# 112 of the 256 pairs are searched, and the gates' reads from DRAM begin four steps later with five steps up to their use

## The chip, the cores and the metric

One NeuronCore of a Trainium2 chip runs one program. The metric is the device time of one execution in microseconds (us). The engines are named as in the profile: PE multiplies matrices, DVE works on vectors, ACT applies functions and copies, POOL issues gathers and some copies, SP issues DMAs, each in the order of its own instructions. They meet at semaphores.

## The reference, cut to what matters

Two transformer blocks on 256 tokens of width 2048. The change lies in the last part of the second block, a product-key expert layer: for each token and each of 8 heads, two lists of 128 scores are cut to the 16 best each, the sums of all 16 x 16 pairs are formed, the 16 best sums are kept, and their softmax weighs 16 of 16384 experts.

```python
sub = jnp.einsum("bshpk,hpnk->bshpn", q, peer_keys).astype(jnp.float32)
s, i = lax.top_k(sub, PEER_TOPK)
cand = (s[..., 0, :, None] + s[..., 1, None, :]).reshape(B, S, PEER_HEADS, PEER_TOPK * PEER_TOPK)
cidx = (i[..., 0, :, None] * N_KEYS + i[..., 1, None, :]).reshape(B, S, PEER_HEADS, PEER_TOPK * PEER_TOPK)
top_s, pos = lax.top_k(cand, PEER_TOPK)
idx = jnp.take_along_axis(cidx, pos, axis=-1)
gate = jax.nn.softmax(top_s, axis=-1).astype(h.dtype)
...
u = jnp.take(peer_u, i_blk, axis=0)
a = jax.nn.gelu(jnp.einsum("td,thkd->thk", x_blk, u)) * g_blk
v = jnp.take(peer_v, i_blk, axis=0)
return jnp.einsum("thk,thkd->td", a, v)
```

Both lists come out of `top_k` in falling order. Pair (a, c), counted from 0, is beaten by every pair with both places no worse, so it can be among the best 16 only where (a+1)(c+1) is at most 16.

## The kernel before, in words

All weights pass through one pipeline. A weight tile `raw` of 1 MB is loaded by SP (L208); ACT rounds half of it to `whi` (L130), DVE forms the rest `wlo = raw - whi` (L131), and PE multiplies with both (L263). Such a half is a piece: in the passes below a piece is 10 matmuls of 512 columns. There are three `raw` tiles and four pairs of `whi` and `wlo`, and a piece is prepared three pieces ahead of its matmuls (`LOOK = 3`).

The dense part of the expert layer multiplies with all experts. A group is 8 pieces (512 experts), a pass U(e) is 4 groups, and its output goes through GELU into a ring (`turn`, L1624 to L1627). After U(0) to U(3) passes V(0), U(4), V(1), ... follow. The gate of every expert multiplies the ring before its V pass. Half of the tokens' second tile goes another way, by gathered rows (`sparse`, L1576 to L1598).

Side work is written as Python generators. After each piece `tick` lets every running generator go `rate` steps on; a step ends at a `yield`. So the order of all instructions is fixed when the program is built, in pieces, and does not depend on time. These matter here:

- `lists_gen` (rate 1) finds the 16 best of each list, with `top16` (L1474 to L1478): five DVE instructions, each over the whole list.
- `top_gen` (rate 1.3) forms the sums (L1513), searches them head by head with `top16`, and finds the two places of each winner by comparing with 0 to 15, multiplying and summing (L1531, L1534, L1536), once for each of two halves of the tokens.
- `g_gen` (rate 0.8) turns the winners into a gate for every expert and writes them to DRAM, `scratch`, in 24 blocks through ACT (L1678) and POOL (L1679).
- `r_gen(e)` reads the gates of V pass e back in three parts of 512 KB (L1687, issued by SP) into one tile `t`, and multiplies the ring with each (L1692, DVE). Reads and multiplies alternate; the next `r_gen` begins when the one before has ended.
- `sparse` begins at the same tick as the first `r_gen`. Its L1576 makes an operand that SP copies between partitions (L1577); then it gathers rows (POOL, L1581) and reduces them (DVE, L1596).

Of the kernel before, what the change touches and what calls it, by code (L numbers as in the profile page):

```python
# [8 lines left out]
H16 = mybir.dt.float16  # L9
# [3 lines left out]
OP = mybir.AluOpType  # L13
# [44 lines left out]
class Builder:  # L58
# [21 lines left out]
    def H(self, i, key, dt=FT):  # L80

        s, n = (i // 2, 4096) if i >= 8 else (10 + i, 2048)
        if self.halves.get(s, (None,))[0] != key:
            self.halves[s] = key, self.pool.tile([128, n], dt, name=f"s{s}_{key}", tag=f"s{s}")
        o = 2048 * (i % 2) if i >= 8 else 0
        return self.halves[s][1][:, o:o + 2048]
# [850 lines left out]
def phase3(b, C, W, gs, X, ident, transposes, residual, norm_of, stat2, act_pair, lhs_of, res_need, bcast, jits,  # L937
# [6 lines left out]
    V, A, G, PE = nc.vector, nc.scalar, nc.gpsimd, nc.tensor  # L944
# [493 lines left out]
    def post_pq(n):  # L1438
        def f(p):
            if n == 0:  # L1440
                for h in range(2):
                    gs["res3", h].drain()
                norm_of(r3, ss3)
                nc.gpsimd.dma_start(H(16, "k")[:, :], d["keysT"])
                for r, lo in ((rd, 0), (rsp, 64)):
                    for o in (0, 64):
                        nc.gpsimd.dma_start(r[o:o + 64, :], r3[lo:lo + 64, 1:2])
                nc.gpsimd.dma_start(fold, d["fold"])
            for h in range(2):
                A.activation(Qp(n, h), b.ps[p.banks[h][0]][:, :], AF.Copy, scale=r3[:, h:h + 1])  # L1450
            gs["key", n] = b.start(key_gen(n))
            gs["lists", n] = b.start(lists_gen(n))
            if n == 2:
                gs["fuse"] = b.start(fuse())
            if n == 3:
                gs["top"] = b.start(top_gen(), 1.3)
        return f
# [7 lines left out]
    iota = C("iota")  # L1465

    def sarr16():

        t = H(7, "g")[:, 1024:2048].bitcast(H16)
        return (t[:, 0:256], t[:, 256:512], t[:, 512:1024].rearrange("p (q t) -> p q t", q=2),  # L1470
                t[:, 1024:1280].rearrange("p (n t) -> p n t", t=2))

    def top16(vals, idx, src, tmp):
        V.max(vals[:, 0:8], src)  # L1474
        V.max_index(idx[:, 0:8], vals[:, 0:8], src)
        V.match_replace(tmp, vals[:, 0:8], src, -3.0e38)
        V.max(vals[:, 8:16], tmp)
        V.max_index(idx[:, 8:16], vals[:, 8:16], tmp)  # L1478

    def found():  # L1480

        t = H(12, "top")
        return t[:, 0:512], t[:, 512:1024].bitcast(U32), t[:, 1024:1536], [t[:, 1536 + i * 256:1792 + i * 256] for i in range(2)]
# [11 lines left out]
    def top_gen():  # L1495
        V16, I16, If, rep = found()
        while not gs["lists", 3].done:
            yield
        V.tensor_copy(If, I16)
        yield  # L1500
        t8 = H(8, "sub")
        T16 = t8[:, 0:128]
        Pi, Pa, Pb = (t8[:, k * 128:k * 128 + 128].bitcast(U32) for k in (1, 2, 3))
        Fa, Fb, E = t8[:, 512:640], t8[:, 640:768], t8[:, 768:1152]
        sm = t8[:, 1152:1160]
        cand, eq = H(16, "k")[:, :], H(17, "k")[:, :]
        i1, i2, g12, it2 = sarr16()
        V.tensor_copy(it2, iota[:, :, None].to_broadcast([128, 128, 2]))
        for h in range(2):
            v4 = V16[:, h * 256:h * 256 + 256].rearrange("p (m q k) -> p m q k", m=8, q=2)  # L1510
            f4 = If[:, h * 256:h * 256 + 256].rearrange("p (m q k) -> p m q k", m=8, q=2)
            for m in (0, 4):
                V.tensor_tensor(cand[:, m * 256:m * 256 + 1024].rearrange("p (m a c) -> p m a c", m=4, a=16),  # L1513
                                v4[:, m:m + 4, 0, :, None].to_broadcast([128, 4, 16, 16]),
                                v4[:, m:m + 4, 1, None, :].to_broadcast([128, 4, 16, 16]), op=OP.add)
                yield
            for m in range(8):
                top16(T16[:, m * 16:m * 16 + 16], Pi[:, m * 16:m * 16 + 16], cand[:, m * 256:m * 256 + 256],
                      rep[m % 2])
                yield  # L1520
            V.tensor_scalar(Pa, Pi, 4, None, op0=OP.logical_shift_right)
            V.tensor_scalar(Pb, Pi, 15, None, op0=OP.bitwise_and)
            V.tensor_copy(Fa, Pa)
            V.tensor_copy(Fb, Pb)
            yield
            for q, F in enumerate((Fa, Fb)):
                for m in (0, 4):
                    e1 = eq[:, m * 256:m * 256 + 1024]
                    e3 = e1.rearrange("p (s a) -> p s a", a=16)
                    e4 = e1.rearrange("p (m s a) -> p m s a", m=4, s=16)  # L1530
                    V.tensor_tensor(e3, F[:, m * 16:m * 16 + 64, None].to_broadcast([128, 64, 16]),  # L1531
                                    iota[:, None, 0:16].to_broadcast([128, 64, 16]), op=OP.is_equal)
                    yield
                    V.tensor_tensor(e4, e4, f4[:, m:m + 4, q, None, :].to_broadcast([128, 4, 16, 16]), op=OP.mult)  # L1534
                    yield
                    V.tensor_reduce(E[:, q * 128 + m * 16:q * 128 + m * 16 + 64], e3, axis=AX.X, op=OP.add)  # L1536
                    yield
            g = E[:, 256:384].rearrange("p (m s) -> p m s", m=8)
            t3 = T16.rearrange("p (m s) -> p m s", m=8)
            V.tensor_tensor(g, t3, t3[:, :, 0:1].to_broadcast([128, 8, 16]), op=OP.subtract)  # L1540
            A.activation(g, g, AF.Exp)
            V.tensor_reduce(sm, g, axis=AX.X, op=OP.add)
            V.reciprocal(sm, sm)
            V.tensor_tensor(g, g, sm[:, :, None].to_broadcast([128, 8, 16]), op=OP.mult)
            if h:
                t = t8[:, 1160:1288].bitcast(I32)
                V.scalar_tensor_tensor(t, E[:, 0:128], 128.0, E[:, 128:256], op0=OP.mult, op1=OP.add)
                V.tensor_copy(which[64:128], t[64:128, 0:64])
                V.tensor_copy(share[64:128], E[64:128, 256:320])
                nc.gpsimd.dma_start(which[0:64], t[64:128, 64:128])  # L1550
                nc.gpsimd.dma_start(share[0:64], E[64:128, 320:384])
            for _ in range(4):
                yield
            p = b.bank()
            for k in range(3):
                PE.transpose(p[:, k * 128:k * 128 + 128], E[:, k * 128:k * 128 + 128], ident)
            s = slice(h * 128, h * 128 + 128)
            V.tensor_copy(i1[:, s], p[:, 0:128])
            V.tensor_copy(i2[:, s], p[:, 128:256])
            V.tensor_scalar(g12[:, 0, s], p[:, 256:384], GSCALE, None, op0=OP.mult)  # L1560
            V.scalar_tensor_tensor(g12[:, 1, s], p[:, 256:384], GSCALE, g12[:, 0, s], op0=OP.mult, op1=OP.subtract)
            yield
        gs["G"] = b.start(g_gen(), GATE_RATE)
# [42 lines left out]
    def ring(e, h):  # L1606

        j = e % 4
        return v3(H(14 + j // 2, "rc")[:, j % 2 * 1024:j % 2 * 1024 + 1024] if h else H(10 + j, "ra")[:, :], 16)
# [20 lines left out]
    def post_U(n):  # L1630

        def f(p):
            if n and ("s", n - 1) in gs:
                gs["s", n - 1].drain()
            for h in range(2):
                A.activation(GT(h), b.ps[p.banks[h][0]][:, :], AF.Copy, scale=rd if h else r3[:, 0:1])
            gs["s", n] = b.start(turn(n))
            if n % 4 == 3:
                gs["R", n // 4] = b.start(r_gen(n // 4))
        return f  # L1640
# [41 lines left out]
    def r_gen(e):  # L1682
        while not (gs["s", 4 * e + 3].done and "G" in gs and gs["G"].done and (e == 0 or gs["R", e - 1].done)):
            yield
        t = H(7, "g")[:, 1024:2048]
        for j in range(3):
            nc.sync.dma_start(t.rearrange("p (k m) -> p k m", k=8),  # L1687
                              b.scratch[8 * j:8 * j + 8, :, 128 * e:128 * e + 128].rearrange("k p m -> p k m"))
            for _ in range(5 if e else 3):
                yield  # L1690
            R = ring(e, j // 2)[:, :, j % 2 * 64:j % 2 * 64 + 64].rearrange("p n (k t) -> p k n t", k=8)
            V.tensor_tensor(R, R, t.rearrange("p (k n t) -> p k n t", k=8, n=16), op=OP.mult)  # L1692
            yield
# [217 lines left out]
```

## Time and profile before

| what | us |
|---|---|
| median of 3 runs | 3228.13 |
| lowest and highest | 3226.35, 3237.43 |
| profiled execution, its own time | 3225.99 |
| its span, first to last instruction | 3224.2 |
| PE busy in it | 3142.5 |
| DVE busy in it | 2249.8 |
| ACT busy in it | 1674.1 |

Busy times are sums over the whole span, and the stages have different limits. The passes U(0) to U(3) lie at about 1895 to 2280 us, the search by `top_gen` at about 1930 to 2050, `g_gen` at about 2050 to 2165, and the reads of the gates from 2171 on.

### The profile page before, as it was taken

Reading aid. Unit: us, or ns where it says so; the run is one execution under the profiler, and the core shown is the slowest. Engines: PE = TensorE matmul, PEld = TensorE weight load, DVE = VectorE, ACT = ScalarE, POOL = GpSimd, SP = SyncE. Lnnn points to the kernel's source line nnn. Section 1 sums busy time; section 2 is a strip of 40 time slices with the busy share of each in tenths; the row PEclk is TensorE's granted clock in tenths of the full one; section 3 lists DMA queues with packets and bytes.
Section 4 is the critical chain, followed back from the end, with each engine's and each line's share of the span. In section 5 each row is a group of like instructions: output and inputs, shape, how many; then the busy total and the mean of one; then the engine's idle time right before and its main releaser. Section 6 shows DMA issues by size and latency. Waiting matters only on the chain.

```text
span 3224.2 us, 37826 instructions
## 1 busy us (share of the span) xinstructions
PE 3142.5 (97%) x14264; PEld 2464.3 (76%) x14264; DVE 2249.8 (70%) x2963; ACT 1674.1 (52%) x2374; POOL 375.7 (12%) x252
## 2 busy tenths in 40 slices
PE   8799999999999999999999998998999999999998
PEld 6677778888888888877787886776777777777776
DVE  6986554444555555654455589987989899999975
ACT  5356454444454455455544554684445554555554
POOL 1011110000000010000000200012121232422300
PEclk9899999999999999999999999999999999999999
DMA  6444455455555546444355554689999999999964
GB/s 230 159 173 169 170 186 183 180 183 183 186 192 184 191 153 220 183 150 151 136 189 180 189 178 170 235 281 347 389 377 383 390 371 398 374 402 368 365 222 163
DMA packets 135239, 768.52 MB, mean 238 GB/s; under 512 B 13008, under 2 KB 38016, under 8 KB 47568
## 3 DMA queue, kind: packets, MB, share of 16 engines
q1 hardware_dynamic: 110000, 604.81, 51.7%
q0 software_dynamic: 24768, 160.25, 12.6%
q8 instruction: 111, 1.82, 0.2%
q10 hardware_dynamic: 288, 1.05, 0.1%
q14 instruction: 72, 0.59, 0.0%
HBM read 750.82 MB, written 14.68 MB: 237 GB/s over the span
## 4 chain that ended last, share of the span: by engine, by line
PE 83%; DVE 9%; DMA 4%; issue 2%; ACT 2%; POOL 0%; SPq 0%; POOLq 0%; ACTq 0%; DVEq 0%
PE ps L263 77%; DVE wlo L131 3%; DVE s_conv L511 1%; DMA raw<-in_peer_u 1%; DMA s_g<-scratch 1%; PE ps L476 1%; ACT whi L130 1%; DMA raw<-in_peer_v 1%; PE ps L1251 1%; PE ps L1624 0%; DMA raw<-in_w_in 0%; PE ps L1250 0%; DVE s_gb L1596 0%; DVE s_x L717 0%; PE ps L1676 0%
## 5 line engine op out<-in xcount | busy, mean ns | idle before, releaser
L131 DVE TENSOR_TENSOR wlo<-raw,whi 128x1024 fp32r<-128x1024 f32 (+2 forms) x1101 | 1330.9, 1217 | 792.5 <-ACT whi L130 787.1
L130 ACT ACTIVATE whi<-raw 128x1024 fp32r<-128x1024 f32 (+2 forms) x1113 | 1164.8, 1051 | 1035.5 <-PE ps L263 729.9
L263 PE MATMUL ps<-whi,s_x 128*128 128x512 f32 (+2 forms) x2816 | 903.2, 396 | 10.7 <-ACT whi L130 6.3
L263 PEld LDWEIGHTS ps<-whi,s_x 128*128 128x128 f32 x2816 | 529.4, 189 | 136.7 <-issue 8.2
L263 PE MATMUL ps<-whi,s_h 128*128 128x512 f32 x1760 | 608.4, 402 | 0.0
L263 PE MATMUL ps<-wlo,s_x 128*128 128x512 f32 (+2 forms) x1408 | 551.8, 392 | 16.8 <-DVE wlo L131 16.8
L263 PE MATMUL ps<-whi,s_vj 128*128 128x512 f32 x1536 | 530.6, 400 | 3.5 <-DVE s_vj L131 2.3
L263 PE MATMUL ps<-wlo,s_h 128*128 128x512 f32 (+1 forms) x1136 | 453.8, 400 | 20.2 <-DVE wlo L131 19.9
L263 PEld LDWEIGHTS ps<-whi,s_h 128*128 128x128 f32 x1760 | 333.8, 190 | 100.1 <-issue 0.8
L263 PE MATMUL ps<-wlo,s_vj 128*128 128x512 f32 (+1 forms) x1024 | 403.9, 394 | 0.2 <-DVE wlo L131 0.2
L263 PEld LDWEIGHTS ps<-whi,s_vj 128*128 128x128 f32 x1536 | 289.3, 189 | 104.8 <-DVE s_vj L131 4.4
L263 PEld LDWEIGHTS ps<-wlo,s_x 128*128 128x128 f32 x1408 | 266.0, 189 | 75.0 <-DVE wlo L131 18.5
L263 PE MATMUL ps<-whi,s_fj 128*128 128x512 f32 x1024 | 322.0, 395 | 0.0
L263 PEld LDWEIGHTS ps<-wlo,s_h 128*128 128x128 f32 (+1 forms) x1136 | 187.4, 165 | 75.0 <-DVE wlo L131 28.2
L263 PEld LDWEIGHTS ps<-whi,s_fj 128*128 128x128 f32 x1024 | 192.2, 188 | 47.4
L263 PE MATMUL ps<-wlo,s_fj 128*128 128x512 f32 x512 | 202.4, 395 | 0.0
L263 PEld LDWEIGHTS ps<-wlo,s_vj 128*128 128x128 f32 (+1 forms) x1024 | 165.1, 161 | 45.8 <-DVE wlo L131 1.3
L1581 POOL DMA_INDIRECT s_k<-in_v_rows,vec x43 | 112.4, 2613 | 208.4 <-DVE s_sp L1598 190.3
L131 POOL TENSOR_TENSOR s_head<-raw,s_head 128x1024 fp32r<-128x1024 f32 x6 | 18.1, 3030 | 892.8 <-ACT s_head L130 892.8
L263 PEld LDWEIGHTS ps<-wlo,s_fj 128*128 128x128 f32 x512 | 96.1, 188 | 22.5
L1598 DVE SCALAR_TENSOR_TENSOR s_sp<-s_k,misc,s_sp 128x2048 f32<-128x2048 f32 x43 | 100.8, 2344 | 0.0
L511 DVE SCALAR_TENSOR_TENSOR s_conv<-s_u,vec,s_conv 128x256 f32<-128x256 f32 x240 | 98.7, 475 | 0.0
(330 smaller groups left out, 2819.2 us busy)
## 6 DMA issues: line engine op xcount, KB each, us to landing
raw<-in_peer_u SPq DMA_DIRECT2D x128, 1024.0 KB, 7.5
raw<-in_peer_v SPq DMA_DIRECT2D x128, 1024.0 KB, 7.6
raw<-in_w_in SPq DMA_DIRECT2D x101, 1024.0 KB, 4.8
raw<-in_w_up SPq DMA_DIRECT2D x64, 1024.0 KB, 4.8
raw<-in_w_down SPq DMA_DIRECT2D x64, 1024.0 KB, 4.8
raw<-in_w_out SPq DMA_DIRECT2D x32, 1024.0 KB, 4.8
raw<-in_w_pq SPq DMA_DIRECT2D x16, 1024.0 KB, 4.8
scratch<-s_k POOLq DMA_DIRECT2D x24, 512.0 KB, 4.4
```

What stands on the lines that cost most here:

```text
L130: nc.scalar.activation(hi, src, AF.Copy)
L131: (engine or nc.vector).tensor_tensor(lo, src, hi.bitcast(FT), op=OP.subtract)
L263: nc.tensor.matmul(self.ps[p.banks[h][b]][:xs[q].shape[-1], :w], xs[q], (wl if q == 1 else wh)[:, s], start=p.first and c == 0 and q == 0, ...
L476: PE.transpose(p[:, k * 256 + h * 128:k * 256 + h * 128 + 128], src(h)[:, col + (c + k) * 128:col + (c + k + 1) * 128], ident)
L511: V.scalar_tensor_tensor(o, src, w, o, op0=OP.mult, op1=OP.add)
L1251: PE.matmul(oo, qp()[r, head // 2, h * 128:h * 128 + 128], kpe()[r, :n], start=False, stop=True)
L1581: nc.gpsimd.indirect_dma_start(buf[g % 3], None, d["v_rows" if g // 64 else "u_rows"], at)
L1598: V.scalar_tensor_tensor(Y(), t, a, Y(), op0=OP.mult, op1=OP.add)
```

## The change

The sums are formed for 112 pairs per head instead of 256: all 16 partners of the first list's four best, and the four best partners of the other twelve, laid out as 64 + 48 in one row of 112. All heads are formed in one step (two instructions) instead of two steps (one instruction each). `top16` then runs over 112 numbers. A place in the row of 112 has to be decoded into two places, which takes seven more small DVE instructions for each half. Lists, places and the compared numbers become 16-bit, so the compare and multiply work on 16-bit data. One step is saved at the sums and one is added at the decoding, so `top_gen` has as many steps as before.

In `r_gen` the first read waits four more steps, and the reads of e = 0 stand five steps ahead of their multiplies instead of three.

```diff
@@ top_gen
-            for m in (0, 4):
-                V.tensor_tensor(cand[:, m * 256:m * 256 + 1024].rearrange("p (m a c) -> p m a c", m=4, a=16),
-                                v4[:, m:m + 4, 0, :, None].to_broadcast([128, 4, 16, 16]),
-                                v4[:, m:m + 4, 1, None, :].to_broadcast([128, 4, 16, 16]), op=OP.add)
-                yield
+            c8 = cand[:, 0:896].rearrange("p (m n) -> p m n", m=8)
+            V.tensor_tensor(c8[:, :, 0:64].rearrange("p m (a c) -> p m a c", a=4),
+                            v4[:, :, 0, 0:4, None].to_broadcast([128, 8, 4, 16]),
+                            v4[:, :, 1, None, :].to_broadcast([128, 8, 4, 16]), op=OP.add)
+            V.tensor_tensor(c8[:, :, 64:112].rearrange("p m (a c) -> p m a c", a=12),
+                            v4[:, :, 0, 4:16, None].to_broadcast([128, 8, 12, 4]),
+                            v4[:, :, 1, None, 0:4].to_broadcast([128, 8, 12, 4]), op=OP.add)
+            yield
             for m in range(8):
-                top16(T16[:, m * 16:m * 16 + 16], Pi[:, m * 16:m * 16 + 16], cand[:, m * 256:m * 256 + 256],
-                      rep[m % 2])
+                top16(T16[:, m * 16:m * 16 + 16], Pi[:, m * 16:m * 16 + 16], c8[:, m], rep[m % 2][:, 0:112])
                 yield
             V.tensor_scalar(Pa, Pi, 4, None, op0=OP.logical_shift_right)
-            V.tensor_scalar(Pb, Pi, 15, None, op0=OP.bitwise_and)
+            V.tensor_scalar(Pb, Pi, 2, None, op0=OP.logical_shift_right)
             V.tensor_copy(Fa, Pa)
             V.tensor_copy(Fb, Pb)
+            V.tensor_copy(Fp, Pi)
             yield
-            for q, F in enumerate((Fa, Fb)):
+            V.scalar_tensor_tensor(Fa, Fb, -12.0, Fa, op0=OP.add, op1=OP.max)
+            V.tensor_scalar(Fb, Fa, -4.0, -48.0, op0=OP.mult, op1=OP.add)
+            V.scalar_tensor_tensor(Fb, Fa, -16.0, Fb, op0=OP.mult, op1=OP.max)
+            V.tensor_tensor(Fb, Fb, Fp, op=OP.add)
+            F16 = [f.bitcast(H16)[:, 0:128] for f in (Pa, Pb)]
+            V.tensor_copy(F16[0], Fa)
+            V.tensor_copy(F16[1], Fb)
+            yield
+            for q, F in enumerate(F16):
                 for m in (0, 4):
-                    e1 = eq[:, m * 256:m * 256 + 1024]
+                    e1 = eq[:, m * 256:m * 256 + 512].bitcast(H16)
...
                     V.tensor_tensor(e3, F[:, m * 16:m * 16 + 64, None].to_broadcast([128, 64, 16]),
-                                    iota[:, None, 0:16].to_broadcast([128, 64, 16]), op=OP.is_equal)
+                                    iota16[:, None, :].to_broadcast([128, 64, 16]), op=OP.is_equal)
@@ r_gen
         t = H(7, "g")[:, 1024:2048]
+        for _ in range(0 if e else 4):
+            yield
         for j in range(3):
...
-            for _ in range(5 if e else 3):
+            for _ in range(5):
                 yield
```

The order on PE, ACT and POOL is the same in both kernels, row for row; only DVE and SP differ. In the rows below the numbers behind `wlo_`, `whi_` and `raw_` are those of the buffers, and line numbers are each kernel's own. First DVE, where `top_gen` begins. Before:

```order
L131 TENSOR_TENSOR wlo_80<-raw_75,whi_76 128x1024
L1499 CAST s_top<-s_top 128x512
L1508 CAST s_g<-cst 128x256
L1513 TENSOR_TENSOR s_k<-s_top 128x1024
L131 TENSOR_TENSOR wlo_81<-raw_75,whi_77 128x1024
L1513 TENSOR_TENSOR s_k<-s_top 128x1024
L131 TENSOR_TENSOR wlo_82<-raw_73,whi_78 128x1024
L1474 MAX s_sub<-s_k 128x8
```

The same place in the changed kernel:

```order
L131 TENSOR_TENSOR wlo_80<-raw_75,whi_76 128x1024
L1500 CAST s_top<-s_top 128x512
L1508 CAST s_sub<-cst 128x16
L1511 CAST s_g<-cst 128x256
L1518 TENSOR_TENSOR s_k<-s_top 128x8x64
L1521 TENSOR_TENSOR s_k<-s_top 128x8x48
L131 TENSOR_TENSOR wlo_81<-raw_75,whi_77 128x1024
L1474 MAX s_sub<-s_k 128x8
```

The sums take one step, so the first search stands one piece earlier. Second, DVE where the gates' first multiply (L1692, in the changed kernel L1710) stands beside the start of `sparse` (L1576, in the changed kernel L1592). Before:

```order
L131 TENSOR_TENSOR wlo_83<-raw_75,whi_79 128x1024
L131 TENSOR_TENSOR wlo_80<-raw_73,whi_76 128x1024
L1692 TENSOR_TENSOR s_ra<-s_ra,s_g 128x8x16x8
L1576 TENSOR_TENSOR s_sp<-s_x,s_sp 64x2048
L131 TENSOR_TENSOR wlo_81<-raw_73,whi_77 128x1024
L131 TENSOR_TENSOR wlo_82<-raw_74,whi_78 128x1024
L131 TENSOR_TENSOR wlo_83<-raw_74,whi_79 128x1024
```

The same place in the changed kernel, up to the multiply:

```order
L131 TENSOR_TENSOR wlo_80<-raw_73,whi_76 128x1024
L1592 TENSOR_TENSOR s_sp<-s_x,s_sp 64x2048
L131 TENSOR_TENSOR wlo_81<-raw_73,whi_77 128x1024
L131 TENSOR_TENSOR wlo_82<-raw_74,whi_78 128x1024
L131 TENSOR_TENSOR wlo_83<-raw_74,whi_79 128x1024
L131 TENSOR_TENSOR wlo_80<-raw_75,whi_76 128x1024
L1612 ISA s_gb,misc<-s_gb,s_sp 128x2048
L1612 ISA misc 128x1
L131 TENSOR_TENSOR wlo_81<-raw_75,whi_77 128x1024
L131 TENSOR_TENSOR wlo_82<-raw_73,whi_78 128x1024
L1710 TENSOR_TENSOR s_ra<-s_ra,s_g 128x8x16x8
```

The multiply went from the place ahead of L1576 to six pieces later, behind the first reduction of gathered rows. Third, SP at the first reads of the gates. Before:

```order
L208 DMA raw_74<-in_peer_u 128x2048
L1687 DMA s_g<-scratch 128x8x128
L208 DMA raw_75<-in_peer_u 128x2048
L1577 DMA s_sp<-s_sp 64x2048
L208 DMA raw_73<-in_peer_u 128x2048
L1687 DMA s_g<-scratch 128x8x128
```

In the changed kernel:

```order
L208 DMA raw_74<-in_peer_u 128x2048
L208 DMA raw_75<-in_peer_u 128x2048
L1593 DMA s_sp<-s_sp 64x2048
L208 DMA raw_73<-in_peer_u 128x2048
L1705 DMA s_g<-scratch 128x8x128
L208 DMA raw_74<-in_peer_u 128x2048
L208 DMA raw_75<-in_peer_u 128x2048
L208 DMA raw_73<-in_peer_u 128x2048
L1705 DMA s_g<-scratch 128x8x128
```

The first read went behind the copy between partitions and behind two more weight loads, and the second is three weight loads after it instead of two. Later reads follow at the same distance of three loads in both kernels; the series ends about five weight loads later.

## Rows read from the trace of the kernel before

**Rows 1.** The page, part 1: busy us, share of the span, instructions.

```profile
PE 3142.5 (97%) x14264; PEld 2464.3 (76%) x14264; DVE 2249.8 (70%) x2963; ACT 1674.1 (52%) x2374; POOL 375.7 (12%) x252
```

**Rows 2.** Busy time by stretch; last three columns: granted PE clock, DMA share, GB/s.

```profile
1930.00:2000.00 70.00, 63.66 (x287) 47.39 (x287) 66.85 (x123) 34.69 (x40) 0.00 (x0) 1.00 0.51 183
2000.00:2060.00 60.00, 55.60 (x240) 41.04 (x239) 57.68 (x108) 29.58 (x36) 1.60 (x3) 0.94 0.51 186
2060.00:2160.00 100.00, 96.61 (x691) 74.62 (x690) 92.80 (x122) 77.55 (x85) 11.17 (x21) 1.00 0.80 277
2160.00:2200.00 40.00, 33.35 (x164) 25.47 (x163) 19.85 (x19) 22.76 (x26) 8.44 (x8) 0.87 0.82 295
2200.00:2280.00 80.00, 74.69 (x334) 55.65 (x333) 71.35 (x65) 36.72 (x47) 22.34 (x14) 1.00 0.97 379
2280.00:2400.00 120.00, 116.46 (x503) 87.79 (x502) 109.87 (x124) 60.33 (x85) 25.08 (x17) 0.99 0.98 375
2400.00:3000.00 600.00, 599.72 (x2661) 458.19 (x2659) 553.27 (x551) 323.86 (x450) 184.59 (x89) 1.00 0.98 384
```

**Rows 3.** Waits of PE, 1930 to 2060 us: total, times, longest.

```profile
PE ps L263 <- DVE wlo L131: 10.4, 10, 3.0
```

**Rows 4.** DVE in order of time: start us, duration us, instruction.

```profile
1925.44 0.29 DVE L1474 MAX8 s_top<-s_sub 128x8 f32<-128x128 f32 x1
...
1927.02 1.21 DVE L131 TENSOR_TENSOR wlo<-raw,whi 128x1024 fp32r<-128x1024 f32 x1
...
1931.38 1.22 DVE L1513 TENSOR_TENSOR s_k<-s_top 128x1024 f32<-128x1024 f32 x1
1932.52 1.22 DVE L131 TENSOR_TENSOR wlo<-raw,whi 128x1024 fp32r<-128x1024 f32 x1
...
1939.30 0.42 DVE L1474 MAX8 s_sub<-s_k 128x8 f32<-128x256 f32 x1
...
1941.55 0.41 DVE L1474 MAX8 s_sub<-s_k 128x8 f32<-128x256 f32 x1
...
1960.62 0.22 DVE L1521 TENSOR_SCALAR s_sub<-s_sub 128x128 uint32<-128x128 uint32 x1
1960.76 0.22 DVE L1522 TENSOR_SCALAR s_sub<-s_sub 128x128 uint32<-128x128 uint32 x1
```

**Rows 5.** DVE groups by shape, 1880 to 2400 us: count, busy us, mean ns.

```profile
L1534 DVE TENSOR_TENSOR s_k<-s_k,s_top 128x1024 f32<-128x1024 f32 x8 | 9.8, 1219 | 0.1
L1665 DVE TENSOR_TENSOR s_k<-s_k,s_g 128x1024 f16<-128x1024 f16 x12 | 8.3, 692 | 0.4
L1544 DVE TENSOR_TENSOR s_sub<-s_sub 128x128 f32<-128x128 f32 x2 | 0.6, 291 | 0.1
```

**Rows 6.** The chain that ended last, in U(0): start, us.

```profile
1918.57 0.84 PE ps L1624 x8
1919.41 11.73 PE ps L263 x50
```

**Rows 7.** DVE at the gates' reads: start, duration, [idle before, what ended it].

```profile
2185.86 1.23 DVE L1692 TENSOR_TENSOR s_ra<-s_ra,s_g 128x1024 f32<-128x1024 f32 x1 [9.60 <-DMA s_g<-scratch]
...
2198.63 1.22 DVE L1692 TENSOR_TENSOR s_ra<-s_ra,s_g 128x1024 f32<-128x1024 f32 x1 [3.52 <-DMA s_g<-scratch]
...
2212.35 1.23 DVE L1692 TENSOR_TENSOR s_rc<-s_rc,s_g 128x1024 f32<-128x1024 f32 x1 [3.53 <-DMA s_g<-scratch]
...
2258.75 1.23 DVE L1692 TENSOR_TENSOR s_rc<-s_rc,s_g 128x1024 f32<-128x1024 f32 x1 [1.75 <-DMA s_g<-scratch]
```

**Rows 8.** SP and PE in order of time at the first read.

```profile
2171.88 0.38 SPq L1687 DMA_DIRECT2D s_g<-scratch  x1
2173.88 0.80 SPq L208 DMA_DIRECT2D raw<-in_peer_u  x1
2189.49 0.53 SPq L1577 DMA_DIRECT2D s_sp<-s_sp  x1
2190.71 0.80 PE L263 MATMUL ps<-wlo,s_h 128*128 128x512 f32 x1 [6.64 <-DVE wlo L131]
```

**Rows 9.** All 24 reads of the gates (L1687), from issue to landing.

```profile
DMA to landing us min/median/max: 7.3/8.9/14.0
```

More of the change, by code (lines that the diff above doesn't have):

```diff
@@ L1498, in top_gen @@
             yield
+        If = If[:, 0:256].bitcast(H16)
         V.tensor_copy(If, I16)
@@ L1505, in top_gen @@
         sm = t8[:, 1152:1160]
+        Fp, iota16 = t8[:, 1288:1416], t8[:, 1416:1424].bitcast(H16)
+        V.tensor_copy(iota16, iota[:, 0:16])
         cand, eq = H(16, "k")[:, :], H(17, "k")[:, :]
```

## The prediction

> **What bounds the kernel now.** I read the page first: PE is busy for 3142.5 us of a span of 3224.2 [rows 1]. What a change in side work can give back is therefore in PE's 82 us of idle time and in stretches at a slower clock, and the question is how much of both lies where this change acts. The busy time by stretch answers it [rows 2]. The reader should subtract the PE column from the length: during the search PE idles 6.34 us in 1930 to 2000 and 4.40 in 2000 to 2060, where DVE is busy for 66.85 of 70 and 57.68 of 60 us. Around the first reads of the gates it idles 6.65 us in 2160 to 2200 and 5.31 in 2200 to 2280, and there DVE is not full (19.85 of 40 us in the first). From 2400 to 3000 PE idles 0.28 us of 600. So the two places have different causes, and time won at either stays won: PE sets the pace of everything behind, and no later stretch has idle time that would absorb it.
>
> The waits of PE name the first cause: in 1930 to 2060 it waited 10.4 us for `wlo`, up to 3.0 at once [rows 3]. `wlo` and the search share DVE's queue. For the second, DVE's order of time shows a 9.60 us wait for the read of the gates [rows 7], and behind that instruction stood L1576 and the next `wlo`; PE then waited 6.64 us for that `wlo` [rows 8]. SP was held too: L1577 needs L1576, went out at 2189.49, and the last weight load before it had gone at 2173.88 [rows 8].
>
> **Part 1, the search.** Times from start to start show what an instruction really takes of DVE. A search of 256 numbers takes 1941.55 − 1939.30 = 2.25 us, one of 128 numbers 1927.02 − 1925.44 = 1.58 [rows 4]. By that slope 112 numbers take 1.50, and 16 searches save 16 × 0.75 = 12.0 us. The sums take 1.14 us of the queue for 1024 numbers [rows 4], four times; in their place stand 512 and 384 numbers per half. The busy times of 128 and 1024 numbers, 291 and 1219 ns [rows 5], lie 1.04 ns per number apart, so these cost about 0.61 and 0.47, and 4.56 − 2.16 = 2.4 us go. A 16-bit multiply of 1024 numbers should cost what L1665 shows, 692 ns against 1219 for L1534 [rows 5]; in the queue that is some 0.70 against 1.14, and eight of them save 3.5. Added are seven small instructions per half: four with one source at 0.14 (1960.76 − 1960.62 [rows 4]) and three with two sources, which I put at 0.21 because their busy time is 0.07 longer (291 against 220 ns [rows 4, 5]); with one cast that is 2 × 1.19 + 0.1 = 2.5. The reduction L1536 I leave as it is, between nothing and the 0.44 that the multiply gains, eight times: no row shows a 16-bit reduction, and its output stays 32-bit. DVE loses 12.0 + 2.4 + 3.5 − 2.5 = 15.4 us of work.
>
> One unknown is the 16-bit compare, whose winner is repeated 16 times in a row. The 16-bit rows that I have [rows 5] read neighbouring numbers only. Its bounds are 1.14 us (as now) and 0.70; I take the first, and the second would take 3.5 us more off DVE. The Trainium skill, VectorE: DVE Perf Modes, section "What auto-detection actually checks", says that the packed mode wants every tensor to be 16-bit and to advance by one element. A repeated element does not, so by that page the compare gains nothing; by the rows alone it could be either.
>
> What PE gets of it: 50 matmuls take 11.73 us, so a piece takes 2.35, and with the transposes (0.84 a group for one tile [rows 6], the other taken alike, over 8 pieces) 2.55. Per piece DVE must do one `wlo` (1.14) and 1.3 steps. With searches that was 1.14 + 1.3 × 2.25 = 4.07, 1.5 too much; eight searches last 6.2 pieces, so DVE falls 9.3 us behind. Preparing three pieces ahead hides some 3 us, and 6.34 us of idle time were left in the first. Now it is 1.14 + 1.3 × 1.50 = 3.09: 0.54 too much, 3.3 us in all, about what is hidden. I leave 1.2 us per search, because sometimes two searches stand between two `wlo`. In the steps that find the places it was 1.14 + 1.3 × 1.14 = 2.62, above 2.55, and becomes 1.14 + 1.3 × 0.99 = 2.43: DVE catches up. The second half also shows a granted clock of 0.94 over 60 us [rows 2]: 3.6 us of full speed, some of it in time that was idle anyway; I count 2.2. Part 1 gives 6.34 + 4.40 + 2.2 − 2.4 = **10.5 us**, between 5 (half of it) and 14.3 (all idle time and clock).
>
> **Part 2, the reads.** The first multiply moves behind six `wlo`, L1576 and one reduction, so L1576 and L1577 run at once, and the weight loads behind L1577 no longer wait for a read. The first read is issued behind two more weight loads. Its landing took 7.3 to 14.0 us [rows 9]; five steps are 5 × 2.55 = 12.8. Reads that had five steps before left DVE waiting at most 1.75 us [rows 7], those of e = 0 9.60, 3.52 and 3.53. What stands behind a late multiply now is a reduction and a `wlo` that has three pieces of lead. So the gap of 6.64 us goes. With it goes part of the slow clock: 0.87 over 40 us is 5.2 us [rows 2], of which a part was idle and a part lies ahead of the gap, and I count 1.9. Of the two 3.5 us waits I count 1.5 of the 5.31 us idle in 2200 to 2280. Against it I put 2.0 for short waits at the new places. That is **8.0 us**. The lower bound is 1.5, if transfers take the place of the wait. The upper one comes from the transfers: 2160 to 2280 moved 295 × 40 + 379 × 80 = 42.1 MB, which at the 384 GB/s of 2400 to 3000 [rows 2] takes 110 us instead of 120; one read fewer in the stretch adds 1.4, so 11.5.
>
> The later reads come five weight loads later, the last of one series falling into U(4) instead of V(0). That costs nothing as long as PE stays as full as in 2280 to 2400 (116.46 of 120 us); without that cover one read of 0.52 MB at 384 GB/s would cost 1.4. The one cast to 16 bits that replaces L1499 costs the same as before.
>
> **Sum.** 3225.99 − 10.5 − 8.0 = 3207.5 us in terms of the profiled execution, which lies 2.1 us below the median of the runs; hence 3209.5. About 0.5% (16 us) is what a measurement of this kernel can tell from no change.
>
> **Rivals.**
> 1. The transfers become the bound of part 2. For it: DMA share is already 0.97 from 2200 on, and 0.82 in the stretch before [rows 2]. Removing the stall pulls weight loads, gathers and reads together. Against it: the same share goes with a full PE from 2400 on. Then part 2 gives 1.5: 3225.99 − 12.0 + 2.1 = 3216. The Trainium skill (Trainium Kernel Development and Optimization, Key Constraints) says that DMAs of the SP, ACT and POOL queues run on the same 16 engines and interleave; by that rule this rival is what to fear, and the shares here agree.
> 2. The search goes on holding PE, because steps with two searches still put 2 × 1.50 + 1.14 = 4.1 us before a `wlo`: half of part 1, 3225.99 − 13.2 + 2.1 = 3215.
> 3. The remaining small gaps in 2200 to 2400 (5.31 + 3.54 us [rows 2]) shrink as well, since each came behind a late read or a late load: 7 us more, 3202.5.
> 4. Slower. The reads stretch, starting now together with the first gathers and the copy L1577. Each of twelve multiplies then holds a reduction and a `wlo`. Five steps and the lead of some 3 us cover 15.8 us, the longest landing was 14.0 [rows 9]. From 17.4 us on the twelve waits cost the whole gain (12 × 1.55); at 17.8 they cost 24 and the time is 3233.
>
> **Chances.** Forecast 0.55 (3204 to 3214), rival 1 0.22, rival 2 0.10, rival 3 0.10, rival 4 0.03. The range 3201 to 3220 takes in both ends of part 2, rivals 1 to 3, and leaves out part 1 and part 2 failing together, and rival 4. Faster by over 0.5% means below 3212: most of the forecast (0.44), rival 3, and a sixth of rivals 1 and 2 (0.05) give 0.59. Slower by over 0.5% is rival 4 at its worst, 0.02. The rest is 0.39.
>
> **What the profile of the changed kernel would show.** If part 1 is right: a search of about 1.50 us from start to start, PE idle near 3 us where `top_gen` runs, a granted clock of 1.00 there, and a multiply (L1534's successor) near 0.70. The compare at 1.2 us or at 0.7 settles the open point. If part 2 is right: no wait above 2 us at the three multiplies of e = 0, L1577's successor issued within 3 us of L1576's end, and no single PE gap above 2 us after `g_gen`. It would be wrong if ACT waited longer for `raw` there (rival 1), if `wlo` still ended waits of PE of 1 us or more in each search (rival 2), or if reads landed after more than 16 us (rival 4).

## Result, and the profile after

The changed kernel takes 3208.44 us (median of 7 runs, 3205.14 to 3214.9); the kernel before, run beside it, 3229.57 (7 runs, 3223.97 to 3237.43). The ratio is 0.9943 with an interval of 0.9932 to 0.9954, so 21 us are gone where 18.6 were forecast; the profiled execution took 3207.39 us. But the two terms of the sum did not come out as worked out: the search gave 5 us more than its term, the reads gave theirs, and a few microseconds were lost again late in the program.

The page of the changed kernel, first part:

```profile
PE 3135.3 (98%) x14264; PEld 2461.9 (77%) x14264; DVE 2235.0 (70%) x2978; ACT 1675.2 (52%) x2374; POOL 371.5 (12%) x252
```

DVE's busy time fell from 2249.8 [rows 1] to 2235.0, with 15 more instructions. The busy time by stretch, same columns and same stretches as [rows 2] (the work in a stretch has moved forward by what was won before it):

```profile
1930.00:2000.00 70.00, 68.84 (x321) 52.98 (x319) 66.27 (x169) 39.12 (x45) 0.00 (x0) 1.00 0.56 207
2000.00:2060.00 60.00, 59.45 (x294) 45.30 (x293) 56.46 (x98) 35.79 (x41) 2.68 (x5) 1.00 0.63 222
2060.00:2160.00 100.00, 95.01 (x688) 73.85 (x687) 87.46 (x112) 80.04 (x88) 14.43 (x25) 1.00 0.79 278
2160.00:2200.00 40.00, 38.99 (x180) 29.85 (x179) 29.20 (x25) 19.28 (x22) 11.19 (x7) 1.00 1.02 372
2200.00:2280.00 80.00, 76.40 (x336) 57.45 (x336) 72.46 (x73) 41.28 (x58) 18.67 (x12) 0.98 1.02 398
2280.00:2400.00 120.00, 117.06 (x517) 88.31 (x516) 111.75 (x119) 59.85 (x80) 25.78 (x18) 1.00 0.99 386
2400.00:3000.00 600.00, 594.24 (x2621) 452.57 (x2620) 549.44 (x550) 321.47 (x449) 186.65 (x87) 1.00 0.97 379
```

PE's idle time (length minus PE) in 1930 to 2060 went from 10.74 to 1.71 us, and in 2160 to 2200 from 6.65 to 1.01; the granted clock is 1.00 in both. DVE is still nearly full where the search runs (66.27 of 70 us): it was relieved, and the time it had left went into matmuls, 321 of them in place of 287 in the first 70 us. The last stretch is the surprise: 5.76 us of idle PE, where there were 0.28.

DVE in order of time, two searches with no `wlo` between them:

```profile
1938.35 0.27 DVE L1474 MAX8 s_sub<-s_k 128x8 f32<-128x112 f32 x1
...
1939.85 0.26 DVE L1474 MAX8 s_sub<-s_k 128x8 f32<-128x112 f32 x1
```

From start to start that is 1.50 us, as forecast (256 numbers: 2.25 [rows 4]). The DVE groups by shape, 1880 to 2400 us: the compare (L1547), the reduction (L1552), a compare of `g_gen` (L1679), the multiply (L1550) and the sums (L1518, L1521):

```profile
L1547 DVE TENSOR_TENSOR s_k<-s_sub 128x1024 f16<-128x1024 f16 x8 | 9.7, 1218 | 0.0
L1552 DVE TENSOR_REDUCE s_sub<-s_k 128x64 f32<-128x1024 f16 x8 | 9.7, 1214 | 0.1
L1679 DVE TENSOR_TENSOR s_gb<-s_g 128x1024 f16<-128x1024 f16 x12 | 8.2, 684 | 0.0
L1550 DVE TENSOR_TENSOR s_k<-s_k,s_top 128x1024 f16<-128x1024 f16 x8 | 5.5, 686 | 0.1
L1518 DVE TENSOR_TENSOR s_k<-s_top 128x512 f32<-128x512 f32 x2 | 1.4, 683 | 0.0
L1521 DVE TENSOR_TENSOR s_k<-s_top 128x384 f32<-128x384 f32 x2 | 1.1, 549 | 0.0
```

The multiply of 16-bit numbers takes 686 ns, the compare of 16-bit numbers 1218, as a 32-bit operation of that size does [rows 5]. That is not because it is a compare: L1679 compares as many 16-bit numbers in 684 ns, and it reads neighbouring numbers from both operands, where L1547 reads one operand's number 16 times in a row. PE's waits from 1930 to 2060 (columns as in [rows 3], where the row says 10.4 us in 10 waits), and below the line of dots those from 2160 to 2280:

```profile
PE ps L263 <- DVE wlo L131: 1.7, 2, 1.2
...
PE ps L263 <- DVE wlo L131: 2.1, 3, 1.0
PE ps L1642 <- ACT s_g L1652: 2.0, 1, 2.0
PE ps L263 <- ACT whi L130: 0.5, 1, 0.5
```

DVE and SP in order of time at the gates' reads, to be held against [rows 7] and [rows 8]:

```profile
2161.18 2.29 DVE L1592 TENSOR_TENSOR s_sp<-s_x,s_sp 64x2048 f32<-64x2048 f32 x1
...
2163.54 0.53 SPq L1593 DMA_DIRECT2D s_sp<-s_sp  x1
...
2165.38 0.38 SPq L1705 DMA_DIRECT2D s_g<-scratch  x1
...
2175.14 2.29 DVE L1612 CUSTOM_DVE_ANT_0 s_gb<-s_gb,s_sp 128x2048 f32<-128x2048 f32 x1 [1.93 <-DMA s_sp<-s_sp]
...
2180.24 1.22 DVE L1710 TENSOR_TENSOR s_ra<-s_ra,s_g 128x1024 f32<-128x1024 f32 x1
...
2198.38 1.23 DVE L1710 TENSOR_TENSOR s_ra<-s_ra,s_g 128x1024 f32<-128x1024 f32 x1 [3.48 <-DMA s_g<-scratch]
...
2212.60 1.23 DVE L1710 TENSOR_TENSOR s_rc<-s_rc,s_g 128x1024 f32<-128x1024 f32 x1 [1.02 <-DMA s_g<-scratch]
```

The first multiply waits for nothing, where it waited 9.60 us [rows 7]. SP's copy goes out 0.07 us after L1592 ends (2161.18 + 2.29 = 2163.47). The second multiply still waits 3.48 us, yet the longest wait of PE in this stretch is 2.0. The three reads of e = 0 took 14.2, 12.9 and 11.2 us to land, where they had taken 14.0, 7.3 and 8.5. All 24 reads, from issue to landing, against [rows 9]:

```profile
DMA to landing us min/median/max: 7.5/9.5/14.2
```

### The profile page after: what moved, and what is told of

Same layout as the page of the kernel before. It is cut to its first block, busy times and chain, and to the rows that moved or that the text cites. A ratio compares the mean times of both kernels' runs of the same rounds, so it can differ in the third digit from the quotient of the medians.

```text
span 3205.6 us, 37841 instructions
## 1 busy us (share of the span) xinstructions
PE 3135.3 (98%) x14264; PEld 2461.9 (77%) x14264; DVE 2235.0 (70%) x2978; ACT 1675.2 (52%) x2374; POOL 371.5 (12%) x252
## 4 chain that ended last, share of the span: by engine, by line
PE 78%; DVE 9%; DMA 6%; issue 4%; ACT 2%; POOL 0%; SPq 0%; POOLq 0%; ACTq 0%; DVEq 0%
PE ps L263 73%; DMA raw<-in_peer_u 3%; DVE wlo L131 3%; DVE s_conv L511 1%; DMA raw<-in_peer_v 1%; PE ps L476 1%; ACT whi L130 1%; DMA s_g<-scratch 1%; DMA scratch<-s_k 1%; PE ps L1251 1%; DMA raw<-in_w_in 1%; PE ps L1250 0%; PE ps L1640 0%; DVE s_x L717 0%; ACT s_k L1694 0%
```

## Experiments

To see where time is won, I use the **lead**. ACT copies each group of 512 experts out of GELU into the ring (`s_ra`); the lead of a kernel at group n is the start of that copy in the profile of the kernel before, minus the start in its own profile. A gain that stays keeps the lead up. U(0) is groups 0 to 3; the two searches lie between groups 1 and 6, the first reads between 10 and 12. ACT in order of time, these copies at groups 1, 6, 10 and 11 in the kernel before:

```profile
1936.27 0.60 ACT L1627 ACTIVATE s_ra<-ps 128x512 f32<-128x512 f32 x1 [1.13 <-PE ps L1626]
...
2056.15 0.60 ACT L1627 ACTIVATE s_ra<-ps 128x512 f32<-128x512 f32 x1
...
2162.85 0.59 ACT L1627 ACTIVATE s_ra<-ps 128x512 f32<-128x512 f32 x1
...
2192.34 0.58 ACT L1627 ACTIVATE s_ra<-ps 128x512 f32<-128x512 f32 x1
```

and in the changed kernel:

```profile
1935.70 0.60 ACT L1643 ACTIVATE s_ra<-ps 128x512 f32<-128x512 f32 x1 [1.14 <-PE ps L1642]
...
2040.05 0.60 ACT L1643 ACTIVATE s_ra<-ps 128x512 f32<-128x512 f32 x1
...
2148.19 0.61 ACT L1643 ACTIVATE s_ra<-ps 128x512 f32<-128x512 f32 x1
...
2169.61 0.58 ACT L1643 ACTIVATE s_ra<-ps 128x512 f32<-128x512 f32 x1
```

So the changed kernel has a lead of 0.57 us ahead of the searches and 16.10 behind them: 15.53 won. At groups 10 and 11 it is 14.66 and 22.73: 8.07 won. The same for every kernel of this study:

| kernel | won, group 1 to 6 | won, 10 to 11 | 11 to 12 | lead at 23 | lead at 31 |
|---|---|---|---|---|---|
| the changed kernel | 15.53 | 8.07 | 0.35 | 24.51 | 19.70 |
| the same once more | 15.53 | 7.36 | -0.83 | 21.21 | 19.67 |
| search alone | 15.56 | -0.54 | 0.07 | 15.78 | 13.81 |
| reads alone | 0.04 | 7.37 | 0.30 | 7.95 | 7.36 |
| later beginning, three steps | 15.57 | 7.43 | -6.54 | 18.90 | 18.87 |
| five steps, no later beginning | 15.57 | 6.73 | -0.19 | 25.84 | 21.96 |
| before, 192 sums searched | 5.29 | 0.00 | -0.07 | 0.73 | 1.67 |
| changed, 32-bit | 11.86 | 7.87 | 0.02 | 20.62 | 20.94 |
| changed, lower rates (e6) | 15.50 | 8.01 | 0.06 | 21.60 | 21.63 |
| before, lower rates (e9) | 0.00 | -0.21 | -0.52 | 1.60 | -0.01 |
| five steps, lower rates (e10) | 15.56 | 7.62 | 1.61 | 26.60 | 25.73 |
| changed, other rates (e11) | 15.53 | 6.79 | 1.86 | 24.73 | 23.24 |

### Each part alone

`e1_search_only` is the changed kernel with `r_gen` as before; `e2_reads_only` is the kernel before with the new `r_gen`.

```diff
 e1, in r_gen of the changed kernel
-        for _ in range(0 if e else 4):
-            yield
...
-            for _ in range(5):
+            for _ in range(5 if e else 3):
 e2, in r_gen of the kernel before
+        for _ in range(0 if e else 4):
+            yield
...
-            for _ in range(5 if e else 3):
+            for _ in range(5):
```

> The search of 112 pairs alone, the reads of the gates as in the kernel before. The lead is the time by which a kernel's profile is ahead of that of the kernel before when ACT copies a finished group to the ring (the GELU of turn): the changed kernel has 16.1 us after the search (group 6), 14.7 at group 10, 22.7 at group 11, 24.7 at group 15 and 19.7 at group 31, the last. Theory A: DVE bounds the whole stretch of the search, so PE gets back all that DVE is relieved of, 15.4 us: a lead of 15 to 16 at group 6, none added at group 11, and 14 to 16 us below the kernel before at the end. Rival B (the forecast's price): what PE gets back is its idle time and part of the slow clock, 10.5 us, and the rest of the 16.1 is chance of one execution: a lead of 10 to 12 at group 6 and 10 to 11 us at the end.

> The search as in the kernel before, the reads of the gates as in the changed kernel. Theory A: nothing at group 6, 8 us at group 11 where the gap of 6.64 us lay, and 8 us below the kernel before at the end, if nothing is given back. Rival: transfers are the bound of what follows and take back 3 to 5 us by group 31, so 3 to 5 us at the end.

The kernel before took 3226.91 beside these two and the next two. The search alone: 3211.92, ratio 0.9952 (0.9933 to 0.997). The reads alone: 3222.19, 0.9983 (0.9971 to 0.9996). That is 15.0 and 4.7 us, 19.7 together, against 21.1 for both in one kernel. The table shows the parts apart: the search wins 15.56 us between groups 1 and 6 and nothing at the reads, the reads 7.37 between groups 10 and 11 and nothing at the search. That is Theory A for the search, in the lead and in the total. For the reads the lead follows it and the total does not: 8 us were expected, 4.7 came, which is where the rival had it. The profiled executions tell when it went: the lead is still 7.36 at group 31, the last, and 4.9 at the end of the program (3224.2 against 3219.3). Part of that is a single wait of PE for ACT, 2.56 us at 3048.69; the kernel before waits 1.2 us there. With the search alone the wait for the first read is as it was, DVE and PE in order of time:

```profile
2172.30 1.23 DVE L1708 TENSOR_TENSOR s_ra<-s_ra,s_g 128x1024 f32<-128x1024 f32 x1 [10.59 <-DMA s_g<-scratch]
...
2177.16 0.80 PE L263 MATMUL ps<-wlo,s_h 128*128 128x512 f32 x1 [7.63 <-DVE wlo L131]
```

### Which half of the edit in `r_gen` does it

`e3_begin_only` is the changed kernel with three steps for e = 0, `e4_steps_only` without the four steps ahead of the first read.

```diff
 e3
-            for _ in range(5):
+            for _ in range(5 if e else 3):
 e4
-        for _ in range(0 if e else 4):
-            yield
```

> The changed kernel with the reads beginning four steps later, but three steps ahead of their multiplies for e = 0 as in the kernel before. Theory A: the first gap is gone, since L1576 no longer stands behind the first multiply, but three steps (7.7 us) are less than the 8 to 14 us that a read takes, so DVE waits 3 to 6 us at each of the three multiplies; PE loses 3 to 5 us of the 8: the lead is some 19 to 21 at group 13 and the time 3 to 5 us above the changed kernel. Rival: only the place of the first multiply counts, and the time is the changed kernel's within 1.5 us.

> The changed kernel with the reads beginning as early as in the kernel before, five steps ahead of their multiplies. Theory A: two more steps already put L1576 ahead of the first multiply, so the gap of 6.64 us shrinks to 0 to 3 (the read takes 14 us there and five steps are 12.8): a lead of 19 to 22 at group 11 and a time 0 to 4 us above the changed kernel. Rival: the first read's being issued among the first gathers is the cause, so the first wait stays above 5 us and the time is 5 us or more above the changed kernel.

Measured: e3 3210.26 (0.9951, 0.9935 to 0.9967), e4 3206.69 (0.9931, 0.9907 to 0.9954). The times alone barely tell them apart, and the 3 to 5 us that e3 was expected to lose against the changed kernel cannot be made out (0.9951 against 0.9943, with overlapping intervals); the profiles do tell them apart. Beginning later alone moves the gap one group on: e3 wins 7.43 us between groups 10 and 11 and loses 6.54 by group 12, where now the late multiply stands. Its DVE and PE:

```profile
2178.77 1.22 DVE L1710 TENSOR_TENSOR s_ra<-s_ra,s_g 128x1024 f32<-128x1024 f32 x1 [5.81 <-DMA s_g<-scratch]
...
2183.40 0.79 PE L263 MATMUL ps<-wlo,s_h 128*128 128x512 f32 x1 [5.87 <-DVE wlo L131]
```

With five steps and no later beginning the first multiply waits 3.10 us,

```profile
2170.17 1.23 DVE L1708 TENSOR_TENSOR s_ra<-s_ra,s_g 128x1024 f32<-128x1024 f32 x1 [3.10 <-DMA s_g<-scratch]
```

but L1592 no longer stands behind it and the pieces prepared ahead cover the rest: the 6.73 us stay. In e3, too, L1592 runs ahead of the first multiply, so its place alone is not what wins the time: there DVE waits 5.81 us with the reduction L1612 and two `wlo` behind the multiply. The five steps, which make the wait short, are what counts; the later beginning adds nothing that these runs can show.

### Is the search's gain all that DVE is relieved of?

PE won 15.5 us where the prediction's upper bound was 14.3 and its account of DVE 15.4. If DVE set the pace of the whole stretch, any microsecond taken from it should come back, one for one. Two kernels change the relief. `e5_192` is the kernel before with searches over the first 192 of 256 sums (64 pairs of each head are left out). `e8_f32` is the changed kernel with 32-bit lists, compare and multiply.

```diff
 e5
-                top16(..., cand[:, m * 256:m * 256 + 256], rep[m % 2])
+                top16(..., cand[:, m * 256:m * 256 + 192], rep[m % 2][:, 0:192])
 e8 (also without the casts and the 16-bit views)
-                    e1 = eq[:, m * 256:m * 256 + 512].bitcast(H16)
+                    e1 = eq[:, m * 256:m * 256 + 1024]
-                                    iota16[:, None, :].to_broadcast([128, 64, 16]), op=OP.is_equal)
+                                    iota[:, None, 0:16].to_broadcast([128, 64, 16]), op=OP.is_equal)
```

> The kernel before, its searches over the first 192 of the 256 sums (so 64 pairs per head are left out of the computation), nothing else changed. By the slope of 5.2 ns per number a search takes 1.92 us instead of 2.25 and DVE is relieved of 16 x 0.33 = 5.3 us. Theory A (DVE bounds the whole stretch, PE gets back what DVE is relieved of): a lead over the kernel before of 5.3 us at group 6, within 0.7. Rival B (PE's idle time is the price, in the forecast's proportion of 10.5 to 15.4): 3.6 us.

> The changed kernel with lists, places, compare, multiply and reduction in 32 bits as in the kernel before. DVE gets 8 multiplies at 1.14 instead of 0.70 us back, and loses five casts: 3.0 us more. Theory A: the lead at group 6 is 3 us less, about 13, and the time some 2 to 3 us above the changed kernel. Rival: in those steps DVE has caught up (2.43 us of work a piece against 2.55 of PE), so PE does not wait for the difference: the lead stays within 1 us.

Between groups 1 and 6 e5 won 5.29 us. Its DVE in order of time:

```profile
1938.54 0.35 DVE L1474 MAX8 s_sub<-s_k 128x8 f32<-128x192 f32 x1
...
1940.45 0.34 DVE L1474 MAX8 s_sub<-s_k 128x8 f32<-128x192 f32 x1
```

A search of 192 numbers takes 1.91 us; 16 × (2.25 − 1.91) = 5.4 us of relief, 5.29 won. e8 gives up 8 × (1219 − 686 ns) = 4.3 us at the multiplies by busy times and is spared five casts, and its lead grows by 3.67 us less than the changed kernel's. The stretch from the copy at group 1 to the copy at group 6 can be summed in each kernel, columns as in [rows 2]: the kernel before, e5, e8, the changed kernel.

```profile
1936.27:2056.15 119.88, 109.14 (x476) 80.52 (x475) 115.15 (x219) 57.49 (x67) 1.60 (x3) 0.97 0.49 176
1935.82:2050.41 114.59, 107.08 (x476) 79.80 (x475) 109.86 (x219) 57.51 (x67) 1.61 (x3) 0.99 0.52 184
1937.84:2045.86 108.02, 104.95 (x476) 78.88 (x475) 103.19 (x222) 57.50 (x66) 1.61 (x3) 1.00 0.56 196
1935.70:2040.05 104.35, 102.63 (x472) 78.46 (x471) 99.51 (x226) 57.62 (x66) 1.60 (x3) 1.00 0.57 203
```

Against the kernel before, DVE is busy for 5.29, 11.96 and 15.64 us less, and the stretch is 5.29, 11.86 and 15.53 us shorter. DVE is idle for 4.7 to 4.8 us in each. One for one, at three sizes; e8's rival, that PE would not wait for the difference, is out. The totals say less: e8 took 3210.51 (0.9941, 0.9924 to 0.9958), e5 3229.5 in one run beside 3230.52 before, and e5's lead fell from 8.58 us at group 19 to 0.73 at group 23, some 500 us after the search, where nothing of its edit acts. Behind group 31 it lost another 5.2 us, where PE waited 5.0 us for ACT at the place of e2's wait of 2.56.

### Where the lead goes later

In the changed kernel the lead falls by 4.8 us between groups 23 and 31. Its waits of PE in 2400 to 3000 us:

```profile
PE ps L1642 <- ACT s_g L1652: 3.5, 3, 1.7
PE ps L263 <- DVE s_vj L131: 2.0, 2, 1.6
```

My idea was that the gathered rows of `sparse`, which run beside this, overload the transfers or DVE. `SPARSE_RATE` says how many steps of `sparse` run at each tick, in U passes and in V passes. `e6_rates` lowers both; `e7_again` is the changed kernel once more, unedited. The rates of `e11_even`, below, are lower in U passes and higher in V passes.

```diff
 e6, e9, e10
-SPARSE_RATE = (0.45, 0.28)
+SPARSE_RATE = (0.42, 0.26)
 e11
+SPARSE_RATE = (0.39, 0.30)
```

> The changed kernel with fewer gathers a piece: rates of 0.42 and 0.26 in place of 0.45 and 0.28; the gathers then end later, in the last V passes. In the changed kernel the lead fell from 24.5 us at group 23 to 19.7 at group 31, and PE idled 5.8 us in 2400 to 3000. Theory A (transfers, at a share of 0.97 to 1.0 of their engines, are the bound there): with 7% fewer gathers the lead stays at 23 to 25 to group 31 and the time is 3 to 5 us below the changed kernel. Rival (the loss is chance of one execution): no difference beyond 1.5 us.

> The changed kernel once more. Theory A (the later loss is a bound): the lead again falls by 3 us or more between groups 23 and 31. Rival (chance): it falls by under 2 us, and the time is that of the changed kernel all the same, within its spread.

e6 took 3201.72 (0.9908, 0.9894 to 0.9922), e7 3207.27 (0.9927, 0.9912 to 0.9942), beside 3230.52. The stretch 2400 to 3000 of e6, columns as above:

```profile
2400.00:3000.00 600.00, 599.17 (x2654) 458.40 (x2653) 543.35 (x552) 331.56 (x455) 147.32 (x82) 1.00 0.97 373
```

and of e7:

```profile
2400.00:3000.00 600.00, 598.17 (x2648) 457.28 (x2647) 554.33 (x553) 325.93 (x453) 185.26 (x88) 1.00 0.98 382
```

The lower rates leave 0.83 us of idle time, but the unedited kernel's second profile shows 1.83 where its first showed 5.76, and its lead falls by 1.5 where the first one's fell by 4.8, as the rival of e7 had it. So what is lost there differs from one execution to another, and one profile doesn't prove the idea. Three more kernels: `e9_before_rates` (the kernel before with the lower rates), `e10_steps_rates` (e4 with them) and `e11_even`.

> The kernel before with the lower rates of gathers alone (0.42 and 0.26); search and reads as before. Theory A (the transfers are a bound that the change came up against: time won upstream lets PE run at full pace into stretches where the transfer engines are at a share of 0.97 to 1.0): in the kernel before PE idled 0.28 us in 2400 to 3000, so lower rates win little, 0 to 2 us below the kernel before. Rival: the gathers disturb both kernels alike, and the lower rates win about as much here as they did on the changed kernel (5.6 us between the medians of the two).

> The changed kernel with the reads beginning as early as in the kernel before (five steps ahead of their multiplies), and the lower rates 0.42 and 0.26. Theory A: the later beginning adds nothing once the five steps are there, so this is the time of the lower rates alone, 3200 to 3203. Rival: beginning early among the first gathers costs when the transfers are relieved otherwise, 3205 or more.

> The changed kernel with rates 0.39 in U passes and 0.30 in V passes. A piece moves 0.52 MB of weights; with 2.55 us a piece in U and 2.35 in V that is an estimate of 366 and 357 GB/s with the gathers, against 390 and 350 at the rates of the changed kernel (0.45 and 0.28). Theory A (transfers bound the U passes): at least as good as the lower rates, 3198 to 3203 us. Rival: V passes, where DVE is at 95%, suffer from the added reductions, and the time is that of the changed kernel, 3206 to 3209.

Beside 3225.29: e9 3223.26 (0.9986, 0.9977 to 0.9995), e10 3202.33 (0.9929, 0.9914 to 0.9944), e11 3203.37 (0.9924, 0.991 to 0.9938). What the lower rates are worth depends on what is compared. e6 beside e7, both against the same runs of the kernel before: 5.6 us between the medians, near the 3 to 5 of its theory, but with a late lead of 21.6 and not of 23 to 25. e9 beside the kernel before: 2.0 us by the medians, 4.5 by the ratio, whose interval is 1.6 to 7.4, so its theory and its rival both stand. e10 beside e4: nothing in the ratios, 0.9929 and 0.9931. e11 came out at the slow end of its theory, with higher rates in V passes. So the lower rates help by something between 0 and 6 us.

That they help by keeping the late lead is not shown. The fall from group 23 to 31 is 0.0 and 0.9 us in e6 and e10 and 1.5 in e11; at the old rates it is 4.8, 1.5 and 3.9 in the changed kernel, e7 and e4, but 0.0 in e3, and in e8 the lead rises by 0.3. And e9, at the lower rates, idles 3.67 us in 2400 to 3000 where the kernel before idles 0.28.

e6 had the lowest median and the lowest ratio of all: the version to keep, though the intervals of e10 and e11 overlap with its own.

## Why the prediction was right, and where its steps were not

**The cause was named rightly.** DVE held PE in the search and a late read held PE at the first multiply; both are gone where they were expected to go, and each part alone wins its own time at its own place.

**What DVE is relieved of, 15.4 us: right in the sum.** DVE was busy for 15.6 us less between groups 1 and 6. The search takes 1.50 and the compare stayed at 1218, both as counted. Two small terms were off and cancelled: behind a 16-bit multiply the next instruction can start after 0.60 to 0.72 us, mostly 0.61, where 0.70 was counted, which is some 0.7 us more in eight; and the seven small instructions take 1.52 us of the queue per half and not 1.19, which is 0.7 less in two. The Trainium skill, VectorE: DVE Perf Modes, section "What auto-detection actually checks", had spoken against a gain at the compare, since the repeated operand does not advance by one element; this trace agrees (1218 against 686 ns for the multiply, whose numbers are neighbours). The reduction, left between nothing and 0.44 us, stayed at 1214 ns with 16-bit input; the section "The perf-mode tier table" of that page gives a reduction only one mode, and the trace agrees.

**What PE gets of it: the term that was mis-sized.** 10.5 us were forecast with an upper bound of 14.3; 15.5 came, beyond the bound. The step that failed is the one that added up PE's idle time and the slow clock and kept 2.4 us back. Printed idle time is less than what a stall costs. PE in the kernel before, in order of time, around three stalls:

```profile
1943.73 0.39 PE L263 MATMUL ps<-wlo,s_h 128*64 128x512 f32 x1
1943.96 0.40 PE L263 MATMUL ps<-whi,s_h 128*128 128x512 f32 x1
1945.04 0.50 PE L263 MATMUL ps<-wlo,s_h 128*128 128x512 f32 x1 [0.69 <-DVE wlo L131]
1945.38 0.62 PE L263 MATMUL ps<-whi,s_h 128*128 128x512 f32 x2
...
1948.41 0.50 PE L263 MATMUL ps<-wlo,s_h 128*128 128x512 f32 x1 [0.78 <-DVE wlo L131]
...
1951.79 0.50 PE L263 MATMUL ps<-wlo,s_h 128*128 128x512 f32 x1 [0.76 <-DVE wlo L131]
```

The matmuls that began behind a wait stand 3.37 us apart, and a piece without a stall takes 2.35 ([rows 6]: 11.73 for five), so each stall cost 1.02 us where 0.78 is printed as idle. The first rows show why: matmuls start 0.23 us apart (1943.73, 1943.96), but the last one ahead of the gap is drawn 0.40 long, and the first one behind it holds the next up for 0.34 (1945.04, 1945.38). And 3.37 us is DVE's own time for a piece there: one search and one `wlo` are 2.25 + 1.14 = 3.39. Ten waits [rows 3] at 0.25 are 2.5 us. With them 10.74 + 3.6 + 2.5 = 16.8, less the 1.7 us of idle time that remain, is 15.1, near the 15.5. That sum is a reckoning and not shown, and its clock term is weak: e9, with the search of the kernel before, needs the same 119.88 us from group 1 to group 6 at a granted clock of 0.99 where the kernel before has 0.97, so a faster clock alone won nothing there. DVE's account needs none of this: where DVE is full and PE waits for it, PE gets back what DVE is relieved of, as the four rows from group 1 to group 6 show.

**Part 2, 8.0 us: right in its main term**, with 8.07 in the first profile and 7.36 and 7.37 in two others, all of it between groups 10 and 11, where the gap of 6.64 us lay. The terms of 1.5 and −2.0 us lie behind that, and no run singles them out. L1592 and SP's copy run at once, as forecast, and e4 shows that five steps do this without the later beginning. "No wait above 2 us at the three multiplies" was wrong: the second waits 3.48 us and costs PE little, because what stands behind it has pieces in hand. "No single PE gap above 2 us" was nearly kept in the first profile, with 2.0 up to 2280 and 2.05 once behind it, and failed in the second (4.17, under the rivals). In the total e2 gained 4.7 us, and the interval of its ratio reaches from 1.3 to 9.4, which takes in the 7.4 of its lead.

**"Time won at either stays won": failed.** The lead was 26.55 us at group 19 and 19.70 at group 31. The ground was that 0.28 us of idle time [rows 2] leave nothing to absorb a gain; but a loss needs no idle time beforehand, and other executions show 1.8 and 5.8 us there. In the first profiled execution this loss and the excess of part 1 are about 5 us each and cancelled in the sum: 18.6 us were won, as forecast, and that this total fits so well is luck. The medians show 21.1, and 23.3 for e7, which loses less late. What makes the loss, and why it differs, stays open.

**The rivals.** Rival 1 (transfers become the bound of part 2) is out as the fate of the whole part: DMA share rose to 1.02 in 2160 to 2280 and the 8 us came anyway, and ACT waited for weight loads as long as before (41.1 us in that stretch, 40.8 in the kernel before). But its sign shows once. At group 14 the lead falls from 24.72 to 21.57 us in the first profile and from 22.05 to 16.70 in that of e7, where ACT waited 6.94 us for a weight load and PE then for ACT:

```profile
2237.05 1.06 ACT L130 ACTIVATE whi<-raw 128x1024 fp32r<-128x1024 f32 x1 [6.94 <-DMA raw<-in_peer_u]
...
2238.74 1.11 PE L1642 MATMUL ps<-cst,s_g 128*128 128x128 f32 x4 [4.17 <-ACT s_g L1652]
```

By group 17 the lead is 25.36 and 20.79 again. Whether transfers make the late loss isn't settled. Rival 2 (search goes on holding PE) is out: one wait of 1.16 and one of 0.53 us remain. Rival 4 needed landings of 17.4 us; the longest was 14.2. Rival 3, more small gaps closing, came in small: idle time in 2200 to 2400 is 3.60 + 2.94 us where [rows 2] has 5.31 + 3.54, 2.3 less where 7 were at stake, and part 2 had already counted 1.5 of it.

## What to carry to other kernels

Where a side engine is full and the main engine waits for it, price a relief by the side engine's own work from start to start, not by the main engine's printed idle time. When a wait is shortened by issuing earlier, look at what stands behind the waiting instruction: here five steps of distance gave all, and starting the series later only moved the gap one group on. Follow the lead group by group before trusting a total: in the first profile two errors of 5 us were hidden in a sum that fitted.

## What the runs showed of the hardware

A stall of PE between matmuls of 512 columns costs about 0.25 us more than the idle time shows (1.02 against 0.78). The copy of half a megabyte between partitions landed after 4.5 us in the kernel before, where the first gathers had landed by then and the DMA share was 0.82, and after 11.4 in the changed one, where it set out together with them at a share of 1.02. The reads of DRAM that followed it were slower too: 12.9 and 11.2 us for the second and third in place of 7.3 and 8.5; over all 24 the median is 9.5 against 8.9. DVE's 16-bit operation of 1024 numbers takes 684 to 686 ns with neighbouring operands, a compare as well as a multiply, and 1218 with one operand repeated, with the same types on both sides.
